# Moving the low weight halves to the front of SBUF: another start address modulo 256 bytes for one of the two stationary operands

## The chip, the cores and the metric

The kernel runs on one core of one Trainium2 chip. The metric is device time in microseconds (us): the median of several executions of the kernel. Profiles come from one execution that was recorded by the hardware profiler. The engines are called as the profile calls them: PE is the matmul engine (PEld its weight loads), DVE the vector engine, ACT the scalar engine, POOL GpSimd, SP the engine that issues the DMAs.

## What is computed

One decoder layer over 304 token columns: 16 meta tokens, 256 prompt tokens and 8 sample sequences of 4 tokens. RMSNorm, one wide input projection that feeds 16 RWKV-7 heads and 4 retention heads, an output projection, then RMSNorm and a SwiGLU feed-forward network (FFN). All weights are float32. Cut to what matters here:

```python
xn = rms_norm(x, norm_mix)
z = xn @ w_in                                   # 2048 x 7456
o_a, S_a = rwkv7_mixer(z[..., :RWKV_COLS], ...)
o_b, S_b = retention_mixer(z[..., RWKV_COLS:], ...)
h = x + concatenate([o_a, o_b], -1) @ w_out     # 2048 x 2048
hn = rms_norm(h, norm_ffn)
h = h + (silu(hn @ w_gate) * (hn @ w_up)) @ w_down   # 2048 x 5632, twice, and 5632 x 2048
y = rms_norm(h, norm_final)
```

## The kernel before, in words

Tokens lie along the free axis. Every big matrix is cut into tiles of 128x128 weights, packed in the order of use into one stream `big`, and read 128x512 at a time (four weight tiles, 2048 bytes in each partition).

A float32 product is made of three faster float32r matmuls. `load` brings 512 columns of raw weights (`wr`, five buffers) with a DMA on SP's queue. `cast` has ACT round them to a float32r high half (`wh`, five buffers); `rest` has DVE write the low half `wl` = `wr` - `wh` (five buffers). The activations are split in the same way into `xh` and `xl` (or, for the down projection, into the two planes of an `act` tile). For each weight tile `main` then issues three matmuls in this order:

```python
self.pe.matmul(acc[:m, :n], hi[:, o:o + m], xh, start=k == 0, stop=False)
self.pe.matmul(acc[:m, :n], hi[:, o:o + m], xl, start=False, stop=False)
self.pe.matmul(acc[:m, :n], lo[:, o:o + m], xh, start=False, stop=k == K - 1)
```

The weights are the stationary operand, which PE loads ahead of each matmul (LDWEIGHTS in the profile); the activations are the moving operand, which streams through. So the load of a low half runs beside the streaming of the matmul before it, `xl` against `wh`, and the next tile's high half is loaded while `xh` streams against `wl`.

The order of the whole program comes from a planner (`Plan`), which models the engines' times in a first pass and replays its decisions in a second. Short jobs (the recurrence, norms, evacuations) are threaded as generators between the matmuls. Its costs don't contain addresses.

**Places in SBUF.** Tiles of `const`, `weights` and `scratch` follow one another in the order in which the pools are opened. In the program as built, `const` begins at byte 16512 of a partition. `xh` and `xl` lead it, each 16 slices of 1280 bytes (5 x 256), and both begin at 128 modulo 256. The pool `weights` holds `wr`, `wh` and `wl`, five buffers of 2048 bytes each, and all fifteen begin at 64 modulo 256. `scratch` holds two arenas in which all other tiles have fixed places: the float32 one at byte 97088, the float32r one at byte 215168, 128 modulo 256.

Where the moving operand begins differs by stage. In the input projection a job takes all 304 columns (start 128 modulo 256), or the 288 from column 16 on (`cols=(META, T)`, start 192), or 290 from column 14 on (start 184). In the output projection, the FFN's gate and up, and the down projection it takes 288 columns from 20 elements into the slice (`SHIFT_X`, `SHIFT_A` = 20, 80 bytes), so it begins at 208 modulo 256, for `act` tiles too.

The change touches `Step.__init__` (the pools) and `cast` (the pool from which `lo` is taken).

Of the kernel before, what the change touches and what calls it, by code (L numbers as in the profile page):

```python
# [9 lines left out]
F32R = mybir.dt.float32r  # L10
# [5 lines left out]
P = 128  # L16
# [31 lines left out]
WS = 5  # L48
# [254 lines left out]
class Timed:  # L303


    def __init__(self, plan, eng, name):
        self._plan, self._eng, self._name = plan, eng, name
# [280 lines left out]
class Step:  # L588


    def __init__(self, tc, I, O, ctx, rooms, draft, log):
        self.tc, self.nc, self.I, self.O = tc, tc.nc, I, O
        self.rooms, self.draft = rooms, draft
        pool = lambda n, b, **k: ctx.enter_context(tc.tile_pool(name=n, bufs=b, **k))
        self.cp = pool("const", 1)
        self.wp = pool("weights", 1)
        self.mp = pool("scratch", 1)
        self.ap_ = pool("acc", ACC, space=bass.MemoryType.PSUM)
        self.pp = pool("psum", 8 - ACC, space=bass.MemoryType.PSUM)
        self.n, self.tags = 0, {}  # L600
        self.plan = pl = Plan(self.nc, rooms, draft, log, (lambda i: i) if draft else tc.keep_in_program_order)
        self.sp = pl.sp
        if not draft:
            self.arena = {dt: self.mp.tile([P, r.size + (GAP if dt == F32 else 0)], dt, tag=f"arena_{dt}", name=f"arena_{dt}")
                          for dt, r in rooms.items()}
        self.pe, self.dve, self.act, self.pool = pl.pe, pl.dve, pl.act, pl.pool
        pl.outside = {v.name for v in (*I.values(), *O.values())}
        self.outs = []
        self.live = 0
        self.done = set()  # L610
# [54 lines left out]

    def cast(self, parts=1):
        hi = self.t([P, 512], "wh", F32R, pool=self.wp, bufs=WS)
        lo = self.t([P, 512], "wl", F32R, pool=self.wp, bufs=WS)
        o = self.halved % WCOLS
        raw = self.raws[0][:, o:o + 512]  # L670
        n = 512 // parts
        part = [slice(c * n, (c + 1) * n) for c in range(parts)]
        for c in part:
            self.act.copy(hi[:, c], raw[:, c])
        self.halves.append((hi, lo))
        self.rests.append((lo, [(lo[:, c], raw[:, c], hi[:, c]) for c in part]))
        self.halved += 512
        if o + 512 == WCOLS:
            self.raws.pop(0)
# [1202 lines left out]
```

## Time and profile before

| what | value |
|---|---|
| median of 3 runs | 1533.62 us (1533.47 to 1534.27) |
| profiled execution, its own time | 1534.83 us |
| its span in the trace | 1533.1 us |
| PE busy | 1516.7 us |
| PEld busy | 1489.5 us |
| DVE busy | 1089.1 us |
| ACT busy | 866.7 us |

Nearly all instructions are issued through one helper, line 314, so rows of the profile are told apart by tiles and shapes and not by lines. `acc<-xh,wl` is a matmul that writes PSUM tile `acc`, with `xh` moving and `wl` stationary; `arena_dt.float32r` as moving operand of `acc` is an `act` tile of the down projection; `mm` are PSUM tiles of the small products. Busy time of a group is the time in which at least one of its instructions ran; matmuls overlap in it, since each is still draining when the next streams.

### The profile page before, as it was taken

How to read it: one execution, taken by the hardware profiler on the slowest of the kernel's cores; microseconds unless marked ns; L12 is line 12 of the kernel's file. 1: busy time of each engine (PE TensorE's matmuls, PEld its weight loads, DVE VectorE, ACT ScalarE, POOL GpSimd, SP SyncE). 2: the span in 40 equal slices, each digit the busy share in tenths (PEclk: the TensorE clock that was granted, in tenths of full speed). 3: DMA queues.
4: the chain of work that ended last, by engine and by line, in shares of the span. 5: the costliest groups of instructions: out<-in, count | busy, mean ns of one | idle time of the engine just before them, and what ended most of it. 6: DMA issues, size and time to landing. Idle time of an engine off the chain costs nothing.

```text
span 1533.1 us, 31919 instructions
## 1 busy us (share of the span) xinstructions
PE 1516.7 (99%) x11446; PEld 1489.5 (97%) x11446; DVE 1089.1 (71%) x2782; ACT 866.7 (57%) x2031; POOL 27.7 (2%) x161
## 2 busy tenths in 40 slices
PE   9999999999999999999999999999999999999997
PEld 8999999999899998999999999999999999999997
DVE  6989789989989877676565565656565656565657
ACT  6775976787886766455444444444444444444446
POOL 1000000000000000000000000000000000000000
PEclk9999999999999999999999999999999999999998
DMA  6544435434444476655555555555555555555553
GB/s 231 174 142 147 125 108 158 122 116 147 166 124 144 165 246 206 219 169 165 168 170 169 175 163 174 166 166 172 167 171 173 166 172 167 171 169 174 165 174 117
DMA packets 136334, 252.33 MB, mean 165 GB/s; under 512 B 15984, under 2 KB 22256, under 8 KB 136176
## 3 DMA queue, kind: packets, MB, share of 16 engines
q1 hardware_dynamic: 136176, 250.29, 54.1%
q8 instruction: 91, 1.49, 0.4%
q14 instruction: 67, 0.55, 0.1%
HBM read 235.95 MB, written 14.28 MB: 163 GB/s over the span
## 4 chain that ended last, share of the span: by engine, by line
PE 93%; DVE 4%; ACT 1%; issue 1%; DMA 0%; SPq 0%; DVEq 0%; ACTq 0%
PE acc L314 82%; PE mm L314 12%; DVE arena_dt.float L314 3%; DVE wl L314 1%; DMA arena_dt.float<-xT 0%; SPq L314 0%; ACT arena_dt.float L314 0%; DVE arena_dt.float32r L314 0%; ACT wh L314 0%; ACT arena_dt.float32r L314 0%; ACT xh L314 0%; DVEq L1878 0%; DVE xl L314 0%; ACT shout L314 0%; DVEq L314 0%
## 5 line engine op out<-in xcount | busy, mean ns | idle before, releaser
L314 PE MATMUL acc<-xh,wh 128*128 128x288 f32 (+2 forms) x2592 | 789.0, 304 | 2.2 <-ACT wh L314 1.4
L314 PE MATMUL acc<-xh,wl 128*128 128x288 f32 (+2 forms) x2592 | 763.9, 295 | 0.3 <-DVE wl L314 0.3
L314 PE MATMUL acc<-xl,wh 128*128 128x288 f32 (+2 forms) x2592 | 763.7, 295 | 0.1
L314 ACT CAST wh<-wr 128x512 fp32r<-128x512 f32 (+1 forms) x827 | 501.5, 616 | 342.7 <-PE acc L314 305.5
L314 DVE TENSOR_TENSOR wl<-wr,wh 128x512 fp32r<-128x512 f32 (+1 forms) x827 | 559.6, 685 | 128.8 <-ACT wh L314 125.9
L314 PEld LDWEIGHTS acc<-xh,wh 128*128 128x128 f32 x2592 | 486.5, 188 | 9.2 <-issue 3.7
L314 PEld LDWEIGHTS acc<-xl,wh 128*128 128x128 f32 x2592 | 486.4, 188 | 4.5 <-issue 1.2
L314 PEld LDWEIGHTS acc<-xh,wl 128*128 128x128 f32 x2592 | 485.6, 187 | 1.0 <-DVE wl L314 0.6
L314 PE MATMUL acc<-arena_dt.float32r,wh 128*128 128x288 f32 x1408 | 275.4, 293 | 0.4 <-ACT arena_dt.float32r L314 0.3
L314 PEld LDWEIGHTS acc<-arena_dt.float32r,wh 128*128 128x128 f32 x1408 | 223.7, 188 | 0.9 <-ACT arena_dt.float32r L314 0.6
L314 PE MATMUL acc<-arena_dt.float32r,wl 128*128 128x288 f32 x704 | 205.9, 293 | 0.0
L314 DVE TENSOR_TENSOR arena_dt.float<-acc,arena_dt.float 128x288 f32<-128x288 f32 (+4 forms) x181 | 72.6, 419 | 164.0 <-PE acc L314 163.7
L314 DVE TENSOR_TENSOR arena_dt.float<-arena_dt.float 128x288 f32<-128x288 f32 (+22 forms) x694 | 174.7, 285 | 11.9 <-ACT arena_dt.float L314 7.6
L314 ACT ACTIVATE arena_dt.float<-arena_dt.float 128x288 f32<-128x288 f32 (+7 forms) x245 | 104.6, 433 | 115.3 <-DVE arena_dt.float L314 113.4
L314 PE MATMUL mm<-arena_dt.float 128*128 128x128 f32 (+7 forms) x1136 | 167.7, 302 | 0.6 <-issue 0.2
L314 DVE TENSOR_TENSOR arena_dt.float<-arena_dt.float,acc 128x288 f32<-128x288 f32 (+1 forms) x210 | 94.4, 450 | 91.9 <-PE acc L314 90.4
L314 PEld LDWEIGHTS mm<-arena_dt.float 128*128 128x128 f32 (+1 forms) x1136 | 141.3, 181 | 11.3 <-issue 3.6
L314 PEld LDWEIGHTS acc<-arena_dt.float32r,wl 128*128 128x128 f32 x704 | 132.1, 188 | 0.0
L314 ACT COPY arena_dt.float<-mm 64x64 f32<-64x64 f32 (+11 forms) x330 | 91.5, 286 | 49.0 <-PE mm L314 44.0
L314 ACT CAST arena_dt.float32r<-arena_dt.float 128x288 fp32r<-128x288 f32 (+4 forms) x73 | 30.6, 424 | 90.1 <-DVE arena_dt.float L314 89.4
L314 ACT COPY arena_dt.float<-arena_dt.float 128x32 f32<-128x32 f32 (+7 forms) x235 | 57.1, 293 | 13.2 <-DVE arena_dt.float L314 11.5
L314 DVE SCALAR_TENSOR_TENSOR arena_dt.float<-arena_dt.float 128x288 f32<-128x288 f32 (+3 forms) x96 | 43.0, 451 | 2.4 <-ACT arena_dt.float L314 0.5
(66 smaller groups left out, 565.5 us busy)
## 6 DMA issues: line engine op xcount, KB each, us to landing
wr<-big SPq DMA_DIRECT2D x823, 256.0 KB, 2.8
arena_dt.float<-s0r SPq DMA_DIRECT2D x16, 512.0 KB, 5.0
out_rts<-arena_dt.float SPq DMA_DIRECT2D x16, 512.0 KB, 4.5
arena_dt.float<-xT SPq DMA_DIRECT2D x4, 576.0 KB, 4.4
arena_dt.float<-lora SPq DMA_DIRECT2D x16, 128.0 KB, 2.6
arena_dt.float<-s0w SPq DMA_DIRECT2D x8, 256.0 KB, 2.9
out_rws<-arena_dt.float SPq DMA_DIRECT2D x8, 256.0 KB, 3.6
out_y<-arena_dt.float SPq DMA_DIRECT2D x7, 288.0 KB, 2.5
```

What stands on the lines that cost most here:

```text
L314: return self._plan.keep(f(*a, **k))
```

## The change

A pool `lows` is opened ahead of all others, and `wl` is taken from it instead of from `weights`.

```diff
+        self.lp = pool("lows", 1)
         self.cp = pool("const", 1)
         self.wp = pool("weights", 1)
         self.mp = pool("scratch", 1)
...
         hi = self.t([P, 512], "wh", F32R, pool=self.wp, bufs=WS)
-        lo = self.t([P, 512], "wl", F32R, pool=self.wp, bufs=WS)
+        lo = self.t([P, 512], "wl", F32R, pool=self.lp, bufs=WS)
```

The five buffers are 10240 bytes, which is 40 x 256. The low halves now begin at 128 modulo 256. `const`, `wr` and `wh` move up by 10240 bytes and so keep their places modulo 256 (`wh` stays at 64); the arenas keep their bytes. No instruction is added, removed or reordered.

## The prediction

> **What bounds the kernel now.** I read the busy times first, then the chain of work that ended last, then its pieces in order of time.
>
> ```profile
> span 1533.1 us, 31919 instructions
> ...
> PE 1516.7 (99%) x11446; PEld 1489.5 (97%) x11446; DVE 1089.1 (71%) x2782; ACT 866.7 (57%) x2031; POOL 27.7 (2%) x161
> ...
> PE 93%; DVE 4%; ACT 1%; issue 1%; DMA 0%; SPq 0%; DVEq 0%; ACTq 0%
> ```
>
> PE is busy for 99% of the span and carries 93% of the chain. A busy PE only says that something was in flight; what counts is how far apart matmuls start. The pieces of the chain give that directly, because a piece is an unbroken run of matmuls with its length and its count (start us, length us, what):
>
> ```profile
> 127.48 7.03 PE acc L314 x51
> ...
> 227.14 5.60 PE acc L314 x42
> ...
> 705.12 789.01 PE acc L314 x6069
> ```
>
> The third piece is the FFN: 6069 matmuls without a gap, 789.01 / 6069 = 130.0 ns each, for 288 columns that begin at 208 modulo 256. The second is a run of the input projection whose jobs take the 288 columns from 192 on: 5.60 / 42 = 133.3 ns. Same shape, same clock, no gap in either, and the moving operand starts 16 bytes lower: 3.3 ns more. The first is a run with 304 columns from 128 on: 7.03 / 51 = 137.8 ns; 130.0 x 304 / 288 would be 137.2, so at most 0.6 ns of it is due to the address. So a start address modulo 256 can change the spacing of these matmuls by about 3 ns, and the spacing is the time of the kernel. That is the only lever that this change can pull.
>
> Does the address above the 256 bytes matter? This is the view of groups by shape, for 800 to 1400 us:
>
> ```profile
> L314 PE MATMUL acc<-xh,wh 128*128 128x288 f32 x1028 | 300.7, 292 | 0.0
> L314 PE MATMUL acc<-xh,wl 128*128 128x288 f32 x1027 | 300.4, 293 | 0.0
> L314 PE MATMUL acc<-xl,wh 128*128 128x288 f32 x1027 | 300.4, 292 | 0.0
> L314 PE MATMUL acc<-arena_dt.float32r,wh 128*128 128x288 f32 x1024 | 199.9, 292 | 0.0
> L314 PE MATMUL acc<-arena_dt.float32r,wl 128*128 128x288 f32 x512 | 149.8, 292 | 0.0
> ```
>
> The columns behind the bar are busy us and mean ns of one. `xh` and `xl` lie at the front of SBUF, the `act` tiles in the float32r arena some 190 KB further on, and the weights rotate through five slots of 2 KB; every mean is 292 or 293 ns. So distance doesn't matter, and what is left is the place modulo 256 bytes.
>
> **The change part by part.** *What moves without a cost.* `wr`, `wh` and the constants go up by 40 x 256 bytes and keep their phase; by the five rows above that is worth nothing. No instruction, DMA or wait is added, `wl` still has five buffers, so no queue sees another order and the planner, whose costs hold no addresses, decides as before.
>
> *DVE's write of the low half.* It now reads at 64 and writes at 128 instead of 64.
>
> ```profile
> L314 DVE TENSOR_TENSOR wl<-wr,wh 128x512 fp32r<-128x512 f32 x823 | 557.9, 686 | 127.3 <-ACT wh L314 124.4
> ```
>
> 686 ns each, and the group stood idle for 127.3 us waiting for ACT's high halves, so in the FFN, where the chain is PE alone, a slower write is covered by that slack. In the input projection the cover is thinner: the chain's list by line gives `DVE wl` 0.9% of the span,
>
> ```profile
> by line: PE acc L314 81.8%; PE mm L314 11.5%; DVE arena_dt.float L314 3.4%; DVE wl L314 0.9%; issue 0.5%; DMA arena_dt.float<-xT 0.3%; SPq L314 0.3%; ACT arena_dt.float L314 0.2%; DVE arena_dt.float32r L314 0.2%; ACT wh L314 0.1%; ACT arena
> ```
>
> or 13.8 us. In three stretches of the trace the mean of this write is 674, 684 and 688 ns, a spread of 2%:
>
> ```profile
> L314 DVE TENSOR_TENSOR wl<-wr,wh 128x512 fp32r<-128x512 f32 x8 | 5.4, 674 | 0.0
> ...
> L314 DVE TENSOR_TENSOR wl<-wr,wh 128x512 fp32r<-128x512 f32 x4 | 2.7, 684 | 0.0
> ...
> L314 DVE TENSOR_TENSOR wl<-wr,wh 128x512 fp32r<-128x512 f32 x384 | 260.2, 688 | 63.0 <-ACT wh L314 61.8
> ```
>
> 2% of 13.8 us is 0.3 us either way. I take zero, since nothing shows that DVE sees the phase at all.
>
> *PE's loads of the low half.* This is where it is decided. The loads:
>
> ```profile
> L314 PEld LDWEIGHTS acc<-xh,wl 128*128 128x128 f32 x2576 | 483.8, 188 | 0.0
> ...
> L314 PEld LDWEIGHTS acc<-arena_dt.float32r,wl 128*128 128x128 f32 x704 | 132.1, 188 | 0.0
> ```
>
> and the matmuls that use them, by shape:
>
> ```profile
> L314 PE MATMUL acc<-xh,wl 128*128 128x288 f32 x1920 | 562.2, 293 | 0.0
> ...
> L314 PE MATMUL acc<-xh,wl 128*128 128x304 f32 x512 | 153.9, 301 | 0.0
> ...
> L314 PE MATMUL acc<-xh,wl 128*128 128x290 f32 x144 | 42.8, 297 | 0.0
> ```
>
> Each low load runs beside the matmul ahead of it, so 2576 + 704 = 3280 spacings are touched, one in three. Of the 1920 with 288 columns, 16 x 16 = 256 are input projection (8 retention q tiles and 8 gate tiles of 16 steps each, start 192); the other 1664 and the 704 of the down projection, 2368 together, start at 208.
>
> For these 2368 the distance from the weights' start to the stream's start goes from 208 - 64 = 144 to 208 - 128 = 80 bytes. The trace has no long run at 80. Bounds: 3.3 ns is the only size of a phase effect that the runs show, so the spacing may go to 133.3 (+7.8 us over 2368), and as nothing excludes a gain, the mirror is -7.8 us. Which value? The nearest rows are the small float32r products of the heads' low-rank matrices, whose weights lie in the arena at 128 or 192 modulo 256 and whose streams start at 0, 64 or 128:
>
> ```profile
> L314 PE MATMUL mm<-arena_dt.float32r 128*128 128x288 f32 x24 | 4.5, 294 | 0.0
> ...
> L314 PE MATMUL acc<-xh,wl 128*128 128x288 f32 x14 | 4.1, 295 | 0.0
> ```
>
> The first is those 24 matmuls over the whole span, 294 ns; the second is the 133.3 ns run at start 192 with weights at 64, 295 ns; the FFN has 292 to 293. A duration rises by about what the spacing does, so other weight phases stay within these 3 ns, none is a cliff. And of the two slow and fast cases, the slow one (192 and 64) has a distance that is a multiple of 64 bytes, the fast one (208 and 64) is 16 off. At 80 bytes it is still 16 off. I take 0 for the 2368, with both ends kept.
>
> In the input projection: 256 spacings at start 192 go from a distance of 128 to 64. Both are multiples of 64, which would leave them; but as they are the slow ones, they have 3.3 ns to win: 0 to -0.8 us, and I take the middle, -0.4. The 512 with 304 columns (start 128) go from a distance of 64 to 0. They have 0.6 ns to win and 3.3 to lose: -0.3 to +1.7 us; I take +0.3, between the middle (+0.7) and nothing, since the small products at other weight phases show no more than 1 to 2 ns. The 144 with 290 columns (start 184): at 3.3 ns, 0.5 us either way, taken as 0.
>
> The sum: 0 - 0.4 + 0.3 + 0 + 0 = -0.1 us of the span of 1533.1 us. The profiled execution took 1534.83 us, 1.7 us around its span and 1.2 us over the median of the runs, which the change doesn't touch. From the median: 1533.62 - 0.1 = 1533.5 us.
>
> The Trainium skill, page "TensorE: Matmul & The Clock Gate", section "Part 2: What happens when you issue a matmul", says that the stream and the weight load have read ports of their own, so that loading the next weights takes nothing from the running matmul, and that warm matmuls follow one another at N / 2.4 + 2.5 ns. For 288 columns that is an estimate of 122.5 ns, and no address is in it. The 130.0 and 133.3 ns above disagree in size, and their difference says that the address does enter. By the page the change is worth exactly nothing; if all of the 7.5 ns above the page's figure hung on the phase of the load beside it, the 2368 spacings could give at most 17.8 us. I use neither.
>
> **The rivals.** *Slower: the low loads collide with the stream.* Mechanism: at start 208 the pair (208, 64) was a lucky one, and (208, 128) behaves like (192, 64). Place: the matmul ahead of each `wl` in the output projection and the FFN, the one that streams the low activations against `wh`. Price: 3.3 x 2368 = +7.8 us, with the input projection's +1.7 at worst; 1541.4 us without it. It decides from 3.1 / 2368 = 1.3 ns per spacing, 3.1 us being 0.2% of the time, about what a measurement of this kernel can tell from no change. For it: the 3.3 ns for 16 bytes are real. Against it: the 16 bytes off a multiple of 64 remain, and the 24 small products with weights at 128 and 192 show 294.
>
> *Faster: high and low loads stand in each other's way.* A load lasts 188 ns, while matmuls start every 130: for 58 ns two loads are in flight. Before, both begin at 64; a low load follows a high one and is followed by a high one, so two of three borders between loads in a tile become borders between different phases. For it: the two rows of 188 against 130.0. Against it: the border between two high loads (`xh,wh` to `xl,wh`) is as before, and the mean of all three kinds of matmul is alike, 292 to 293, as it would be if all collided or none did. Price: if a border costs half of the phase effect, 1.65 ns, 2 x 2368 x 1.65 = -7.8 us, 1525.8 us; at a third of that it gives -2.6 us and is lost in the 0.2%. It decides from 3.1 / 4736 = 0.65 ns a border.
>
> *The change doesn't do what it says:* the pool order shifts the streams too and the 208 is lost. Then all 7104 matmuls (3 x 2368) of these stages would go to 133.3, +23 us. The 10240 bytes are 40 x 256, so I give it next to nothing and count it with the slower case.
>
> **How the numbers follow.** No measurable change: 0.56, for it stand the five equal rows, the 294 of other weight phases and the 16 bytes that stay. Faster, mostly by the loads' borders: 0.24, since two of three borders change and the trace can't tell "all collide" from "none does". Slower, by the collision: 0.20. The likeliest case's own range is the bounds of the small terms, -0.8 - 0.3 - 0.5 - 0.3 = -1.9 and +1.7 + 0.5 + 0.3 = +2.5 us, so 1531.7 to 1536.1. The range for 8 in 10 goes from 1528 (all of no change, and somewhat over half of the faster case, whose price runs from -3 to -8) to 1540 (three quarters of the slower one, +3 to +8).
>
> **What would show each step.** In the profile after, the long FFN piece of the chain: 6069 matmuls in 789 us again, 130.0 ns each. In the collision case it lasts about 6069 / 3 x 3.3 = 6.7 us longer, and `xl,wh` alone is longer, by some 3 ns, in the groups by shape. In the faster case it shortens, and all kinds or those beside a border shorten by 1 to 2 ns. Runs with 288 columns from 192 should stay between 132.2 and 133.3 on average (one spacing in three may win 3.3), and 304 columns near 137.8. `wl<-wr,wh` on DVE should stay at 686 ns. The forecast is wrong if the FFN piece moves by over 3 us, or if the span moves with an FFN piece that stands still; then the place is the input projection, and DVE's part in the chain would say so.

## The result, and the profile after

The changed kernel takes 1525.41 us (median of 6 runs, 1524.77 to 1527.93) against 1533.55 us before (6 runs, 1533.27 to 1534.94). The ratio is 0.9949, 95% interval 0.9936 to 0.9962: faster by half a per cent. The forecast was 1533.5 us and no measurable change, with a range down to 1528; the result lies outside it.

The head of the profile after, and its chain by engine:

```profile
span 1523.3 us, 31919 instructions
...
PE 1506.5 (99%) x11446; PEld 1479.4 (97%) x11446; DVE 1087.7 (71%) x2782; ACT 866.4 (57%) x2031; POOL 27.7 (2%) x161
...
PE 89%; DVE 7%; ACT 2%; issue 1%; DMA 0%; SPq 0%; DVEq 0%; ACTq 0%
```

The same instructions, and 10.2 us less of a busy PE. Where, the pieces of the chain say (start us, length us, what). Before:

```profile
28.21 9.78 PE acc L314 x72
...
611.13 89.69 PE acc L314 x684
...
705.12 789.01 PE acc L314 x6069
...
1496.12 23.99 PE acc L314 x182
```

After:

```profile
26.78 9.82 PE acc L314 x72
...
225.76 5.53 PE acc L314 x42
...
609.82 88.17 PE acc L314 x684
...
702.28 782.29 PE acc L314 x6069
...
1486.56 23.87 PE acc L314 x182
```

The long FFN piece is 6.72 us shorter: 782.29 / 6069 = 128.9 ns a matmul instead of 130.0. The 684 matmuls of output projection and first FFN steps give another 1.52 us, the 182 at the end 0.12. The 684 gained twice as much each: 128.9 ns now too, but 89.69 / 684 = 131.1 before, although they had the same three starts as the FFN's. From the start of the first piece to the start of the 684 the input projection lasts 583.04 us after and 582.92 before, so nothing is gained there. The first piece begins 1.43 us earlier, but that goes with the clock at the start of the run: over the first 26.5 us the mean granted clock is 0.94 in this profile of before and 1.00 in that of after. Of the kernels below, `lo64_mid` and `hi128_lo64` also have 0.94 and begin the piece at 28.4 and 28.5 us; the others have 1.00 and begin it between 26.5 and 27.0, the slow `lo192` among them. Leaving this out, 9.8 - 1.4 = 8.4 us of the span come from the spacing of matmuls that stream from 208, close to the 8.1 us between the medians.

The groups by shape, 800 to 1400 us, after:

```profile
L314 PE MATMUL acc<-xh,wl 128*128 128x288 f32 x1041 | 304.0, 292 | 0.0
...
L314 PE MATMUL acc<-xl,wh 128*128 128x288 f32 x1041 | 302.9, 291 | 0.0
```

Mean durations barely tell: 291 or 292 ns instead of 292 or 293. Distances from start to start do. Worked out from the trace's instruction starts, for the down projection (mean ns from the start of the matmul to the start of the next, by kind, and their sum; `xh` and `xl` stand for the high and low plane of an `act` tile):

```text
kernel                    xh,wh   xl,wh   xh,wl   one weight tile
before   (hi 64, lo 64)   130.0   130.0   130.0   390.0
after    (hi 64, lo 128)  129.2   128.4   129.2   386.8
```

The matmul beside which the low half is loaded (`xl,wh`) gained 1.6 ns, but the other two, whose streams and the loads beside them begin where they began before, gained 0.8 each.

### The profile page after: what moved, and what is told of

Same layout as the page of the kernel before. It is cut to its first block, busy times and chain, and to the rows that moved or that the text cites. A ratio compares the mean times of both kernels' runs of the same rounds, so it can differ in the third digit from the quotient of the medians.

```text
span 1523.3 us, 31919 instructions
## 1 busy us (share of the span) xinstructions
PE 1506.5 (99%) x11446; PEld 1479.4 (97%) x11446; DVE 1087.7 (71%) x2782; ACT 866.4 (57%) x2031; POOL 27.7 (2%) x161
## 4 chain that ended last, share of the span: by engine, by line
PE 89%; DVE 7%; ACT 2%; issue 1%; DMA 0%; SPq 0%; DVEq 0%; ACTq 0%
PE acc L314 79%; PE mm L314 10%; DVE arena_dt.float L314 5%; DVE wl L314 2%; ACT arena_dt.float L314 1%; DMA arena_dt.float<-xT 0%; ACT wh L314 0%; SPq L314 0%; DVE arena_dt.float32r L314 0%; ACT arena_dt.float32r L314 0%; DVE xl L314 0%; ACT xh L314 0%; DVEq L1879 0%; ACT shout L314 0%; DVEq L314 0%
## 5 line engine op out<-in xcount | busy, mean ns | idle before, releaser
L314 PE MATMUL acc<-xh,wh 128*128 128x288 f32 (+2 forms) x2592 | 787.5, 304 | 2.1 <-ACT wh L314 1.3
L314 PE MATMUL acc<-xh,wl 128*128 128x288 f32 (+2 forms) x2592 | 763.2, 294 | 0.3 <-DVE wl L314 0.3
L314 PE MATMUL acc<-xl,wh 128*128 128x288 f32 (+2 forms) x2592 | 760.1, 293 | 0.1
L314 ACT CAST wh<-wr 128x512 fp32r<-128x512 f32 (+1 forms) x827 | 501.2, 616 | 334.6 <-PE acc L314 297.9
L314 DVE TENSOR_TENSOR wl<-wr,wh 128x512 fp32r<-128x512 f32 (+1 forms) x827 | 559.3, 686 | 125.6 <-ACT wh L314 122.7
L314 PEld LDWEIGHTS acc<-xh,wh 128*128 128x128 f32 x2592 | 486.7, 188 | 9.0 <-issue 3.7
L314 PEld LDWEIGHTS acc<-xl,wh 128*128 128x128 f32 x2592 | 486.2, 188 | 4.5 <-issue 1.2
L314 PEld LDWEIGHTS acc<-xh,wl 128*128 128x128 f32 x2592 | 485.3, 187 | 0.9 <-DVE wl L314 0.6
L314 PE MATMUL acc<-arena_dt.float32r,wh 128*128 128x288 f32 x1408 | 273.1, 292 | 0.4 <-ACT arena_dt.float32r L314 0.3
L314 PEld LDWEIGHTS acc<-arena_dt.float32r,wh 128*128 128x128 f32 x1408 | 223.7, 188 | 0.9 <-ACT arena_dt.float32r L314 0.6
L314 PE MATMUL acc<-arena_dt.float32r,wl 128*128 128x288 f32 x704 | 205.6, 292 | 0.0
L314 DVE TENSOR_TENSOR arena_dt.float<-acc,arena_dt.float 128x288 f32<-128x288 f32 (+4 forms) x181 | 72.8, 420 | 161.7 <-PE acc L314 161.4
L314 DVE TENSOR_TENSOR arena_dt.float<-arena_dt.float 128x288 f32<-128x288 f32 (+22 forms) x694 | 175.4, 287 | 11.9 <-ACT arena_dt.float L314 7.6
L314 ACT ACTIVATE arena_dt.float<-arena_dt.float 128x288 f32<-128x288 f32 (+7 forms) x245 | 104.7, 434 | 114.5 <-DVE arena_dt.float L314 112.6
L314 PE MATMUL mm<-arena_dt.float 128*128 128x128 f32 (+7 forms) x1136 | 167.6, 302 | 0.7 <-issue 0.2
L314 DVE TENSOR_TENSOR arena_dt.float<-arena_dt.float,acc 128x288 f32<-128x288 f32 (+1 forms) x210 | 94.6, 451 | 88.3 <-PE acc L314 87.0
L314 PEld LDWEIGHTS mm<-arena_dt.float 128*128 128x128 f32 (+1 forms) x1136 | 141.3, 181 | 11.4 <-issue 3.9
L314 PEld LDWEIGHTS acc<-arena_dt.float32r,wl 128*128 128x128 f32 x704 | 132.1, 188 | 0.0
L314 ACT COPY arena_dt.float<-mm 64x64 f32<-64x64 f32 (+11 forms) x330 | 91.6, 287 | 48.9 <-PE mm L314 39.9
L314 ACT CAST arena_dt.float32r<-arena_dt.float 128x288 fp32r<-128x288 f32 (+4 forms) x73 | 30.5, 423 | 89.4 <-DVE arena_dt.float L314 88.7
L314 ACT COPY arena_dt.float<-arena_dt.float 128x32 f32<-128x32 f32 (+7 forms) x235 | 57.1, 293 | 13.3 <-DVE arena_dt.float L314 11.5
L314 DVE SCALAR_TENSOR_TENSOR arena_dt.float<-arena_dt.float 128x288 f32<-128x288 f32 (+3 forms) x96 | 43.1, 452 | 2.4 <-ACT arena_dt.float L314 0.5
```

The costliest lines, as they stand in the source:

```text
L314: return self._plan.keep(f(*a, **k))
```

## The experiments

Three theories stood at first. **Pair:** the spacing belongs to a load and the stream beside it, by their distance. **Border** (the forecast's "faster" rival): successive loads that begin alike hinder each other. **Place:** it isn't the phase but the new place in SBUF. A fourth came out of the first four runs, **PE's rhythm**: the spacing belongs to the whole repeating sequence of three streams and three loads.

In what follows "64/128" means high halves at 64 and low halves at 128 modulo 256.

**64/64 in a pool of its own** (`lo64_mid`).

```diff
-        self.lp = pool("lows", 1)
         self.cp = pool("const", 1)
+        self.lp = pool("lows", 1)
```

> The low halves keep a pool of their own, but it lies behind the constants, so they begin at 64 modulo 256 as before the change. Pair theory (what counts is the place modulo 256 at which a load and the stream beside it begin) and border theory (what counts is that successive loads begin at different places): both 1533.5 us, long FFN piece 789 us, 130.0 ns a matmul. Place theory (a pool of their own, away from the raw and high halves, is what helped): 1525.4 us, FFN piece 782 us.

Measured: 1534.49 us, ratio 1.0002 [0.9992, 1.0011] to the kernel before.

```profile
705.54 789.01 PE acc L314 x6069
```

The FFN piece is that of before to the hundredth. Another pool and another place with the same phase do nothing; the place theory falls.

**128/128** (`both128`).

```diff
         self.lp = pool("lows", 1)
+        self.hp = pool("highs", 1)
         self.cp = pool("const", 1)
...
-        hi = self.t([P, 512], "wh", F32R, pool=self.wp, bufs=WS)
+        hi = self.t([P, 512], "wh", F32R, pool=self.hp, bufs=WS)
```

> High halves also at 128 modulo 256, in front beside the low ones. Pair theory: the two spacings of a tile that have a high load beside them shorten as the one with a low load did, by 1 to 1.7 ns; FFN piece 770 to 778 us, 1514 to 1521 us in all. Border theory: all loads begin alike again, so the gain is gone: FFN piece 789 us, 1533.5 us.

**128/64, the two swapped** (`hi128_lo64`): `wh` from a pool that is opened first, `wl` from `weights`.

```diff
-        self.lp = pool("lows", 1)
+        self.hp = pool("highs", 1)
...
-        hi = self.t([P, 512], "wh", F32R, pool=self.wp, bufs=WS)
-        lo = self.t([P, 512], "wl", F32R, pool=self.lp, bufs=WS)
+        hi = self.t([P, 512], "wh", F32R, pool=self.hp, bufs=WS)
+        lo = self.t([P, 512], "wl", F32R, pool=self.wp, bufs=WS)
```

> The two swapped: high halves at 128, low halves at 64 modulo 256. Pair theory: two of three spacings have the good load, so more is gained than by the change: FFN piece 774 to 780 us, 1517 to 1523 us. Border theory: the borders are as after the change: FFN piece 782 us, 1525.4 us.

**64/192** (`lo192`): the pool `lows` between two parts of the constants.

```diff
-        self.lp = pool("lows", 1)
         self.cp = pool("const", 1)
+        self.lp = pool("lows", 1)
+        self.cp2 = pool("const2", 1)
...
-        self.half = self.t([P, 4, 8], "half", pool=self.cp)
+        self.half = self.t([P, 4, 8], "half", pool=self.cp2)
```

> Low halves at 192 modulo 256, high halves at 64. Border theory: the loads differ as after the change, 1525.4 us, FFN piece 782 us. Pair theory: the stream begins 16 bytes behind the load instead of 80 or 144, which no run has shown; xl,wh alone is longer or shorter by up to 3.3 ns against before, 1525 to 1541 us, and not the same as after except by chance.

Measured: 1541.12 us (ratio 1.0047 [1.0032, 1.0062]), 1555.39 us (1.0139 [1.0124, 1.0154]) and 1556.81 us (1.0152 [1.0135, 1.0169]). All three are slower than the kernel before. Their FFN pieces, in that order:

```profile
704.11 795.75 PE acc L314 x6069
```

```profile
708.60 805.86 PE acc L314 x6069
```

```profile
706.32 809.23 PE acc L314 x6069
```

131.1, 132.8 and 133.3 ns a matmul. Border theory needed 130.0 for the first and 128.9 for the other two; it falls. Pair theory needed the first faster than the change; instead the pair "`xl` streaming, low half loaded from 128" itself takes 130.8 ns here and 128.4 after the change:

```text
kernel                    xh,wh   xl,wh   xh,wl   one weight tile
both128     (128, 128)    131.6   130.8   130.9   393.4
hi128_lo64  (128, 64)     133.1   131.5   133.8   398.3
lo192       (64, 192)     130.8   135.8   133.3   400.0
```

A pair has no time of its own; it falls too. What is left is the whole sequence, and the question whether PE makes it alone or meets other engines.

**Matmuls alone** (`micro`). The layer gives way to one block of float32r data and the three matmuls of a weight tile, 32 times for each setting of stream start `s`, `hi` and `lo`; ACT, DVE and the DMAs rest meanwhile.

```python
for i, (s, hi, lo, n, m) in enumerate(combos()):
    acc = accs[i % 2]
    xh, xl, wh, wl = at(s, 0), at(s, 1280), at(hi, 4096), at(lo, 5120)
    for k in range(REPS):
        for w, x in (wh, xh), (wh, xl), (wl, xh):
            nc.tensor.matmul(acc[:m, :n], d[:, w:w + m], d[:, x:x + n], 
                             start=k == 0 and x == xh and w == wh, stop=k == REPS - 1 and w == wl)
```

> Matmuls alone: the three matmuls of a weight tile, 32 times over, for 116 settings of stream start, high start and low start modulo 256, from one block of data that is loaded once; the layer itself is left out. PE theory (the spacing is made between PE's own stream and its own weight loads, by the three start addresses together): the five settings that the kernels have had come out as there, 130.0 ns a matmul for stream 208 with halves at 64 and 64, 128.9 for 64 and 128, 131.1 for 128 and 128, 132.8 for 128 and 64, 133.3 for 64 and 192; and moving all three by the same bytes changes nothing. Other-engines theory (ACT, DVE and the DMAs write and read the halves beside PE, and the address decides whom they meet): with these idle the five come out alike, within 0.5 ns of one another. The pair theory, already bent by the last runs, would need the sum of three to be made of one value for each load and stream.

Mean of the 72 spacings from the 24th to the 96th matmul of a setting, from the starts in the trace, beside the long FFN piece of the kernel that has the setting:

```text
stream  hi   lo    bare matmuls   kernel
208     64   64    130.0          130.0  (before)
208     64   128   128.9          128.9  (after)
208     128  128   131.1          131.1  (both128)
208     128  64    132.8          132.8  (hi128_lo64)
208     64   192   133.3          133.3  (lo192)
240     96   160   128.9
```

PE alone gives the spacing of the long FFN piece to a tenth of a nanosecond, so nothing that ACT, DVE or DMAs do is needed for it; for the FFN the other-engines theory falls. The output projection of before is not covered: its 131.1 ns at 208, 64 and 64 came in `lo64_mid` again (89.69 us for the 684), while the bare loop gave 130.0 each time it had this setting, and no run shows why. Moving all starts by 64 bytes left each of 16 stream starts within 0.1 ns. Stream 192 with both halves at 128 gave 132.2 and, at its second place in the run, 131.7, so what ran before a setting can matter. Moving by 32 kept 128.9 (last row), but stream 240 with both halves at 96 gave 131.1, not 130.0, which may be the same effect.

**A map of starts** (`micro2`): the same loop with high halves at 64, 16 stream starts by 8 low starts, and every fifth setting again in reverse order.

> The matmuls alone again (the layer is left out), high halves fixed at 64, all 16 stream starts in steps of 16 bytes by 8 low starts in steps of 32; then every fifth setting once more in reverse order. PE theory: stream 208 has 130.0 at 64, 128.9 at 96 and 128, 133.3 at 192 again; the map lies between 128.5 and 138 ns; a setting gives the same whatever was run before it, within 0.7 ns. Pair theory: the time of a setting is a sum of one term for each load and stream, so that low starts rank alike for all streams after allowing for the distance.

```text
ns      lo 0    32     64     96     128    160    192    224
s 176   131.1  131.1  134.8  133.3  137.8  131.1  131.7  131.1
s 192   133.3  132.6  133.3  131.1  131.1  133.3  132.2  133.3
s 208   132.5  131.1  130.0  128.9  128.9  130.4  133.3  132.2
s 224   131.9  131.1  133.3  132.2  133.3  132.6  132.6  133.3
```

Four of the 16 rows; the whole map lies between 128.9 and 137.8, and the change's setting, with its neighbour at low start 96, is its lowest. The columns rank differently in each row, so there is no sum of one term for each load and stream. Of the 26 settings that ran twice, 21 agreed within 0.15 ns and five differed by 0.4 to 1.5, four of them by more than the 0.7 expected at most. Two settings also differ between this run and the first one: stream 112 with both halves at 64 (130.0 here, 132.5 there) and stream 80 (131.7 here, 130.0 there).

**Back to the kernel with the map: 64/96** (`lo96`) and **all three moved by 32** (`moved32`). As in `lo192`, the pools stand between constants, here behind `omu` (`lo96`), or behind `ones` and `omu` with `SHIFT_X` and `SHIFT_A` at 28 (`moved32`).

```diff
-SHIFT_X = [20] * KT
-SHIFT_A = [20] * 11
+SHIFT_X = [28] * KT
+SHIFT_A = [28] * 11
```

> Low halves at 96 modulo 256 between constants, high halves at 64. PE theory: the bare matmuls gave 128.88 ns at 96 as at 128, so FFN piece 782 us and 1525.4 us, as after the change. Rival (only multiples of 64, or the place at the front of SBUF, do it): FFN piece 789 us or more, 1533 us or more.

> All three moved by 32 bytes against the change: high halves 96, low halves 160, and the stream of output projection and FFN 240 (shift of 28 elements). PE theory: only differences count, bare matmuls gave 128.90 ns, so FFN piece 782 us and about 1525 us. Rival (the absolute start counts): another value, between 780 and 830 us as the bare settings spread.

Measured: 1526.58 us (0.9957 [0.9941, 0.9974]) and, from a single execution, 1525.98 us. The FFN pieces, `lo96` and then `moved32`:

```profile
702.37 782.30 PE acc L314 x6069
```

```profile
703.22 782.30 PE acc L314 x6069
```

Both are the 782.29 of the change to a hundredth. At this setting only differences of starts count, and the bare matmuls foretold the FFN of both kernels.

**What the effect hangs on** (`micro3`): the low activations' start alone, the columns of a load (`m`), the length of a stream (`n`) and the PSUM column of the target.

> The matmuls alone (the layer is left out), with one thing changed at a time: the low activations' stream starts elsewhere than the high one's; loads of 32, 64 and 96 columns instead of 128; streams of 256 to 512 columns; and other columns of the PSUM bank as the target. Load theory (the differences come from a load that reads beside a stream): with 32 columns the settings that lie 129 to 135 ns apart with 128 columns come together within 1 ns, and with 64 and 96 lie between. Rival, the write side (PSUM's address enters): another PSUM column moves the settings by 1 ns or more. Stream-length: if the cost arises where load and stream overlap, the excess over the pure stream stops growing once the stream is longer than the load, about 288 columns; if it arises in the stream itself it grows in proportion to 512. For the low stream's start: values between 128 and 136 ns, and none under 128.5.

PSUM column 16, 64 or 100: 130.0, 128.9 and 133.3 ns for low starts 64, 128 and 192, as at column 0. The write side plays no part. Another start for the low stream alone gives 128.9 to 135.6; 208, the same as for the high stream, is the lowest or within 0.1 ns of it. With loads of 32 columns in place of 128 (the values for 128 are those of `micro4` below):

```text
stream  hi   lo    128 columns   32 columns
208     64   64    130.0         130.0
208     64   128   128.9         131.1
208     128  64    132.8         133.3
208     64   192   133.3         131.1
192     64   64    133.3         130.0
176     64   64    134.6         130.0
```

The settings did not come together within 1 ns, so the load theory as it was put fails: a load of a quarter of the columns changes the rhythm, but takes neither the spread nor the excess over bfloat16's 122.5 ns (`micro4`) away. With 128-column loads the length of the stream gives:

```text
columns          256     288     320     512
208, 64/64       118.6   130.0   148.9   233.3
208, 64/128      119.6   128.9   146.7   231.1
208, 64/192      118.5   133.3   146.7   228.9
```

Over bfloat16's 122.5 and 215.8 ns the excess is 6.4 to 10.8 ns at 288 columns and 13.1 to 17.5 at 512. So it is no fixed cost for each matmul and doesn't stop at the length of a load; but it grows by 1.2 to 2.4 times where the columns grow by 1.8, and from 256 to 288 columns the time grows by 9.3 ns in one setting and 14.8 in another. The order changes as well: the starts of the change are the slowest of the three at 256 columns, and those of `lo192`, the slowest at 288, are the fastest at 512.

**Other types** (`micro4`): the loop with float32r, bfloat16 and float32 data, at the six settings above with 288 columns and three of them with 512.

> The matmuls alone (the layer is left out), the same starts with float32r, bfloat16 and float32 operands, streams of 288 and 512 columns. Rate theory (the excess over the pure stream, and with it the effect of the addresses, is there because a float32r stream asks SBUF for 4 bytes at every column at full speed): bfloat16, with half the bytes, and float32, which the trace of before shows at half the speed, have an excess of a few ns that is the same for all six settings within 0.5 ns and for both lengths; float32r repeats 130.0, 128.9, 132.7, 133.3 ns and the 233 and 231 ns of 512 columns. Rival (a matter of how loads and streams take turns, whatever they read): the settings differ by 1 ns or more in the other types too.

```text
                          288 columns            512 columns
float32r  (6 / 3)         128.9 to 134.6         228.9 to 233.3
bfloat16  (6 / 3)         122.5, all six         215.8, all three
float32   (6 / 3)         485.0, all six         858.3, all three
```

The groups of that run by shape show it too (`a<-h` is bfloat16, `a<-d` float32r, `a<-f` float32, in two passes for each matmul; busy us, mean ns):

```profile
L1886 PE MATMUL a<-f 128*128 128x288 f32 x1152 | 279.5, 406 | 0.0
...
L1886 PE MATMUL a<-d 128*128 128x288 f32 x576 | 76.3, 294 | 0.0
L1886 PE MATMUL a<-h 128*128 128x288 bf16 x576 | 70.7, 286 | 0.0
```

70.7 / 576 is 122.7 ns for each bfloat16 matmul, 76.3 / 576 is 132.5 for float32r, 279.5 / 1152 is 242.6 for each float32 pass. What rate theory forecast came true: addresses matter for float32r, with 4 bytes of every partition for each column, and at these settings not at half the bytes (bfloat16) or about half the pace (float32). A rival is the length of a load. It is 98 ns for bfloat16 (first line), below the spacing, and 188 for float32r in the same run, above it; but 32 columns of float32r load in 108 ns (second line, from `micro`), below every spacing, and the settings with such loads still lie between 130.0 and 133.3.

```profile
L1886 PEld LDWEIGHTS <-h 128*128 128x128 bf16 x864 | 84.5, 98 | 48.2 <-issue 0.3
```

```profile
L1887 PEld LDWEIGHTS a<-d 128*32 128x32 f32 x192 | 20.8, 108 | 4.4
```

The Trainium skill, page "TensorE: Matmul & The Clock Gate", section "Wait — 56ns, not 53.3ns?", gives N / 2.4 + 2.5 ns for warm matmuls, by which 288 and 512 columns come to an estimated 122.5 and 215.8 ns. The bfloat16 loop agrees to 0.1 ns, while float32r lies 6.4 to 12.1 ns above it at 288 columns.

## Why the prediction was wrong, point by point

*What bounds the kernel* held: the spacing of PE's matmuls is the time of the FFN, and a start modulo 256 bytes moves it by a few ns. `lo64_mid`, `lo96` and `moved32` bear out that place and distance in SBUF, new pools and DVE's write cost nothing (`wl<-wr,wh` is 687 ns instead of 686).

*The failed step* is "I take 0 for the 2368". Three things in it were wrong.

First, the reason: "at 80 bytes it is still 16 off" a multiple of 64. With both halves at 64, the bare matmuls gave 130.0 ns at a distance of 144 bytes, 131.1 at 80 and 133.3 at 208 in both runs that had them, and all three are 16 off (16 bytes gave 130.0 in one run and 131.7 in the other). There is no such rule.

Second, the unit. The working charged one spacing in three, the one beside a low load. The change moved all three: per weight tile of the down projection 390.0 became 386.8 ns, and half of that gain is on matmuls with unchanged pairs. Charging pairs looked natural because two rows of before (130.0 and 133.3) could be read as two pairs; they were two sequences.

Third, the nearest row. The 24 low-rank products with 294 ns were read as "no cliff". A mean duration of 24 matmuls in mixed surroundings doesn't resolve the 1.1 ns at stake; the long pieces of the chain do, but they held only the settings of before.

The profile of before also held a sign against pairs that went unread: its 684 matmuls at 131.1 ns (`611.13 89.69 PE acc L314 x684`) have the same starts as the FFN at 130.0.

The end that was kept for the bound, -7.8 us, is about what came, but by luck: 6069 spacings of 1.1 ns and 684 of 2.2 happen to make nearly what 2368 of 3.3 would. The range stopped at 1528 as only half of the faster rival's price was let in.

*The faster rival* had the time (1525.8 us) and foretold that other kinds of matmul would shorten too, but not the cause: `both128`, `hi128_lo64` and `lo192` contradict its loads that begin alike.

*The slower rival* is real for other starts: had the low halves gone to 192 instead of 128, its 133.3 ns would have come true, but as the mean of all three spacings (130.8, 135.8 and 133.3) and so with three times the price (809.23 - 789.01 = 20.2 us in the FFN piece).

*The input projection.* Here too all three spacings of a tile moved, and the forecast's terms (-0.4, +0.3 and 0 us) were off; that their sum was nearly right is luck. From start to start between matmuls of one shape, 288 columns went from 133.4 to 131.5 ns, 304 from 137.8 to 138.4 and 290 from 133.4 to 134.3. Over 768, 1536 and 432 matmuls that is an estimated -1.5, +0.8 and +0.4 us, or -0.3 together. PE's busy time from the first piece to the 684 says the same, 580.5 us before and 580.2 after, so the stage kept its length because PE had next to nothing to give there. (The run of 42 at start 192 went from 5.60 to 5.53 us, 131.7 ns, bare 131.1, somewhat below the 132.2 that the forecast allowed.) The chain by line up to the end of that stage (before to 611 us, after to 609.8):

```profile
by line: PE acc L314 57.0%; PE mm L314 28.3%; DVE arena_dt.float L314 7.5%; DVE wl L314 2.3%; issue 1.3%; DMA arena_dt.float<-xT 0.8%; SPq L314 0.7%; ACT arena_dt.float L314 0.6%; DVE arena_dt.float32r L314 0.4%; ACT wh L314 0.4%; ACT arena
```

```profile
by line: PE acc L314 50.6%; PE mm L314 24.4%; DVE arena_dt.float L314 11.8%; DVE wl L314 3.8%; ACT arena_dt.float L314 3.2%; issue 2.5%; DMA arena_dt.float<-xT 0.8%; ACT wh L314 0.7%; SPq L314 0.7%; DVE arena_dt.float32r L314 0.4%; ACT aren
```

PE's matmuls gave up 10 points of the chain, and DVE and ACT took most of them, although PE worked as long as before: the chain's shares don't measure what an engine gained. Across the change and the first four experiments this stage, from the first piece to the 684, lasts 583.0 to 584.9 us, while the FFN piece ranges from 782 to 809. The longest, 2.0 us over before, is `hi128_lo64`, whose spacings here (304 columns: 140.2 ns) add an estimated 3.3 us, so the stage follows PE in part.

*What stays open* is the mechanism inside PE: what costs a float32r stream its excess, and why the sequence falls into a rhythm that depends on all three starts and, for some settings, on what ran before. Open too is why the output projection of before ran at 131.1 ns. Of the three types tried only float32r shows the effect; the excess is larger at 512 columns than at 288; PSUM's column plays no part, and the FFN's spacing comes without any other engine.

## What to carry to other kernels

Where PE is bound by float32r matmuls, the start addresses of streams and weights modulo 256 bytes are a tuning knob worth some per cent (here -0.9% to +2.6% of the FFN piece), and the knob belongs to the whole repeating sequence, so that it can't be reasoned out pair by pair. A kernel of bare matmuls that goes through the starts foretold the long FFN piece to 0.1 ns, and one run maps a hundred settings. It has to use the stream's own length, since other lengths rank the starts otherwise, and it doesn't carry over to every stage: the input projection's 304 columns took 137.8 to 140.2 ns in the kernels and 137.8 at all four bare settings. Where a stage has several column lengths, the gains of one can be the losses of another.

## What the runs showed of the hardware that was not expected

- A float32r matmul of 288 columns takes 128.9 to 137.8 ns from start to start, by addresses alone; bfloat16 takes 122.5 at all six settings tried.
- The spacing is a cycle of the sequence, not a constant. In the kernel before, matmuls alternate between 129 and 131 ns; with low halves at 192, the one beside the low load takes 131, 132 or 140.
- Some settings have more than one rhythm: 5 of 26 gave another spacing, by up to 1.5 ns, after other neighbours, and in the kernel before the same starts gave 131.1 ns in one stage and 130.0 in the next.
